# Down projection: 32 of its 44 K tiles as seven products over a sliding window of K pairs

## The chip, the cores and the metric

The kernel runs on one core of a Trainium2 chip. The metric is the device time of one execution in microseconds (us), from the first instruction to the last; the median of three runs is quoted. The five engines are named as in the profile: PE (matrix multiply, with its weight loads on a line of its own, PEld), DVE (vector), ACT (scalar), POOL (GpSimd) and SP, which issues most of the transfers.

## The reference, cut to what matters

One layer with two sub-layers is computed for 656 token columns (528 of one prompt stream with its meta tokens, 128 of eight sample streams), of which 640 reach the end. First come RMSNorm, an input projection, two mixers and an output projection; that part is not touched. Then comes the gated MLP:

```python
up = x @ w_up                       # 2048 -> 2 * 5632
g, v = up[..., :D_FF], up[..., D_FF:]
gc = conv_b
for k in range(FFN_CONV_W):         # depthwise causal conv, width 3
    gc = gc + gext[:, k:k + seqlen] * conv_w[k]
h = jax.nn.gelu(gc) * v
return h @ w_down                   # 5632 -> 2048
...
x = x + f                           # residual, then a final RMSNorm
```

In tiles of 128 the hidden width 5632 is 44 K tiles for `w_down`, and the output width 2048 is 16 row blocks n. Everything is float32; the products must be close to float32.

## The kernel before

**Products.** Each float32 operand is split into a rounded high part and a low rest (weights `wh` and `wl`, activations the same), and a product is three matmuls: wh with the high part, wh with the low part, wl with the high part. ACT writes the high part by a cast, DVE writes the low part by a subtraction. The 640 columns go as two halves of 320, so a weight tile costs six matmuls of 320 columns.

**The up projection** (`pu`, the stage ahead of the change) runs by Strassen's and Winograd's scheme: for each of 44 hidden tiles f, seven products (`CHAINS`: A11, P1, A22, P3, P2, A12, P4) over 8 pairs of K tiles replace eight. The activations stand ready in seven combinations (`B11, T1, B21, B22, T2, T3, T4`) in the tile `XT` for pairs 0 to 5 and in seven tiles `XH`, tags `xh0` to `xh6`, for pairs 6 and 7. A unit is half a chain: four weight tiles, 12 matmuls. Of the weights, A11, A21, A22 and A12 are loaded (`Up.load`), and DVE forms the sums P1, P3, P2, P4 (`Up.add`); the halves `wraw` and `wr` hold them. Cast and subtraction (`Up.split`) run three units ahead. Products are evicted by `evict_up`, then `gate` forms h of tile f on DVE and ACT, and POOL stores it to DRAM (`h_d`).

**The down projection** (`md` and `me`, the two names of its PSUM tiles) takes K tiles 0 to 39 in four chunks (`DCH`) of 11, 10, 10 and 9. For each chunk and n, six matmuls per K tile gather in PSUM, and `evict_down` adds the 640 columns into `acc`, which was loaded from `x3_d`, the residual rows in DRAM. `feed` reloads h tiles from `h_d` into a ring (`hida` in the seven `xh` tags, `hidb` in the space that `XT` had) and splits them.

**The tail** takes the last four K tiles (40 to 43) for column ranges of 384 and 256, adds, squares, normalises and stores. It stays as it is.

**Order.** Every engine runs its instructions in the order in which they were written out. The writing-out keeps a clock of its own (`E.now`, advanced by each matmul), and background generators (`E.spawn`, `E.tick`) place evictions, loads and splits where that clock says that their inputs are due. On the chip an engine, or a queue, that waits holds back all that stands behind it.

Of the kernel before, what the change touches and what calls it, by code (L numbers as in the profile page):

```python
# [16 lines left out]
DCH = [list(range(0, 11)), list(range(11, 21)), list(range(21, 31)), list(range(31, 40))]  # L17
# [26 lines left out]
def weight_order():  # L44
    o = []
    for k in range(KD):
        for n in range(4):
            o.append(("in", k, n))
    for n in range(4, 8):
        for k in range(KD):  # L50
            o.append(("in", k, n))
    for g in (3, 2, 1, 0):
        for n in (8 + 2 * g, 9 + 2 * g):
            for k in range(KD):
                o.append(("in", k, n))
# [32 lines left out]
    for k in DCH[0]:  # L88
        for n in range(4):
            o.append(("down", k, n))  # L90
    for c, ks in enumerate(DCH):
        for n in range(0 if c else 4, 16):
            for k in ks:
                o.append(("down", k, n))
# [9 lines left out]
B11, T1, B21, B22, T2, T3, T4 = range(7)  # L104
# [57 lines left out]
class Emit:  # L162
    def __init__(self, tc, A):
# [10 lines left out]
        self.limit = self.order.index(("down", 0, 0)) // CH  # L174
# [103 lines left out]
def body(tc, A):  # L278
# [40 lines left out]
    with tc.manual_schedule():  # L319
# [970 lines left out]
        UN = [(f, c, h) for f in range(NFF) for c in range(len(CHAINS)) for h in range(2)]  # L1290
# [3 lines left out]
        class Up:  # L1294
# [24 lines left out]

            def add(self, u):  # L1320
                if u >= len(UN):
                    return
# [3 lines left out]
                if p == "P1":  # L1326
                    if f:
                        self.put(f, "P1", h, "wraw")
                    else:
                        R[f, "P1", h] = r("A21")  # L1330
                    TT(r("P1"), r("A21"), r("A22"), ADD)
# [12 lines left out]
                if f == NFF - 1 and p == "P2" and h:  # L1344
                    E.limit = E.nchunk
                    for _ in range(4):
                        E.load_raw()

            def free(self, f, name, h):
                if f + 1 < NFF:  # L1350
# [5 lines left out]
            def hi(self, u):  # L1356
                if u < len(UN):
# [4 lines left out]
            def lo(self, u):  # L1362
                if u < len(UN):
# [16 lines left out]
        up.pool, up.later = None, []  # L1380
        pss = [mm4() for _ in range(2)]
# [60 lines left out]
        def f26():  # L1442
            return fpool[0].tile([128, 2 * XW], F32, tag="f26", name="f26", bufs=fpool[1])

        fpool = [None, 8]
# [6 lines left out]
        def gate(f, g, v, bufs=1):  # L1452
# [8 lines left out]
            gc, sq = f26(), f26()  # L1461
# [20 lines left out]
        def early(f, g, v):  # L1482
            while gating[0] < f:
                yield
            yield from gate(f, g, v)
            nc.gpsimd.dma_start(out=h_d[f], in_=v[:, 0:640])
            gating[0] += 1

# [4 lines left out]
        def evict_up(f, c):  # L1493
            a, d, e, cc, b = (PB.get((f, i)) for i in range(5))
            if c == 0:
                T_["m1"] = f7.tile([128, XW], F32, tag="m1", name="m1", bufs=1)
                S.copy(out=T_["m1"], in_=a[:, 0:XW])
            elif c == 4:
# [4 lines left out]
                v = T_["v"] = f26()  # L1503
# [3 lines left out]
                T_["done"] = f  # L1507
            elif c == 5:
                g = T_["g"] = f26().rearrange("p (a c) -> p a c", a=2)
                G.memset(g[:, 1, 320:322], 0.0)  # L1510
                TT(g[:, 0], b[:, 0:XW], T_["m1"], ADD)
            elif c == 6:
                g = T_["g"]
                TT(g[:, 1, 0:320], e[:, 0:320], T_["u2"], ADD)
                E.spawn(early(f, g, T_["v"]))
# [16 lines left out]
        def load_h(f):  # L1532
            hraw[f] = hidtile()
# [13 lines left out]

        mm = T.matmul
        for u, (f, c, h) in enumerate(UN):
            _, ty, bk, acc_ = CHAINS[c]  # L1550
            n = XW if ty in (B11, B21) else 320
# [25 lines left out]
            if u == len(UN) - 1:  # L1577
# [5 lines left out]
            for i in range(4):  # L1583
                k = 4 * h + i
                xh, xl = xkind(k, 0, ty)[:, 0:n], xkind(k, 1, ty)[:, 0:n]
                mm(out=p, lhsT=wh[:, i, :], rhs=xh, start=not acc_ and k == 0, stop=False, **more)
                mm(out=p, lhsT=wh[:, i, :], rhs=xl, start=False, stop=False, **more)
                mm(out=p, lhsT=wl[:, i, :], rhs=xh, start=False, stop=k == KP - 1, **more)
                E.tick()
            if h and u > 1:  # L1590
                E.spawn(evict_up(f, c), 0, True)
            if f == NFF - 1 and h and c < 6:
                load_h(c)
                E.spawn(first_h(c, E.now + 6))


        while (NFF - 1, 6) not in evicted:
# [10 lines left out]
        passed = [-1]  # L1608
        D = {}

        def feed():
            while gating[0] < NFF:
# [5 lines left out]
            fpool[1] = 8  # L1618
            D.update(cms=(cm_l1, cm_f8), acc=lps[0].tile([128, 16, 640], F32, name="acc"),
                     ssq=fpool[0].tile([128, 640], F32, name="ssq3"))  # L1620
            due = {}

            def load(f):
                if f < NFF:
                    while f - RING > passed[0]:
                        yield
                    load_h(f)
                    due[f] = E.now + 7

            for f in range(6, 9):  # L1630
                yield from load(f)
# [4 lines left out]
            for f in range(6, NFF):  # L1636
                yield from load(f + 3)
                yield from E.until(due[f])
# [22 lines left out]
        def down(c, ns):  # L1661
            ks = DCH[c]
            pss = {n: mm4() for n in ns}
            for k in ks:
                while k not in hid:
                    E.tick(True)
                for n in ns:
                    E.wtile(("down", k, n), pss[n][0], hid[k][:, 0], hid[k][:, 1], HP, k == ks[0], k == ks[-1])
            for n in ns:
                evict_down(n, pss[n][1])  # L1670

        for c, ks in enumerate(DCH):
            if c == 0:
                down(0, range(4))
            for n in range(0 if c else 4, 16):
                if c == len(DCH) - 1 and n == 12:
                    while NFF - 1 not in hid:
                        E.tick(True)
                down(c, [n])
            for k in ks:  # L1680
                hid.pop(k)
            passed[0] = ks[-1]
# [105 lines left out]
def _lay_out(x_prompt, x_sample, state_ssm_re, state_ssm_im, state_pool, state_ffn_conv,  # L1788
# [13 lines left out]
    for i, o in enumerate(order):  # L1802
        if o[0] == "pool":
            wts[i // CH, :, i % CH] = wp[o[1], o[2], :, o[3]]
        else:
# [4 lines left out]
                           for f in range(NFF) for k, n in ((0, 0), (0, NFF), (1, NFF), (1, 0))]).reshape(-1, 128, 4, 128)  # L1810
    xp = np.concatenate([meta_tokens, x_prompt[0]], axis=0)
# [52 lines left out]
```

## Time and profile before

| | us |
|---|---|
| median of three runs (2378.72 to 2382.51) | 2381.11 |
| the profiled execution | 2380.44 |
| its span on the core | 2378.7 |
| PE busy | 2335.2 |
| DVE busy | 1657.4 |
| ACT busy | 944.0 |
| POOL busy | 353.4 |

The span is what the profile sees of the profiled execution; 1.7 us of its time lie around it. The kernel has a first part of some 640 us with short waits, the up projection from 645.6 to 1739.9 us, the down projection from there to 2303.4 us, and a tail. Busy time of PE is a share of the span and says nothing of how fast single matmuls follow each other; that is read from how many start in a stretch.

### The profile page before, as it was taken

The page shows a single profiled execution, that of the slowest core. Times are in us where ns is not written, and L with a number is a line of the kernel's source. Part 1 is how long each engine was busy: PE and PEld are TensorE (multiplying, and loading weights), DVE is VectorE, ACT ScalarE, POOL GpSimd, SP SyncE. Part 2 cuts the span into 40 slices and gives each one's busy share as a digit, 9 for nine tenths or more (in the row PEclk, how much of TensorE's full clock was granted, in tenths as well). Part 3 has the DMA queues.
Part 4 walks back from the last instruction along what each step waited for, and adds up shares of the span by engine and source line. Part 5 has one row for each costly group of instructions (what it writes and reads, how often), then busy time and mean ns, then how long its engine had stood idle before and what let it go on. Part 6 is the DMA issues. An engine that isn't in the chain of part 4 may idle for free.

```text
span 2378.7 us, 41101 instructions
## 1 busy us (share of the span) xinstructions
PE 2335.2 (98%) x15824; PEld 2325.1 (98%) x15824; DVE 1657.4 (70%) x2709; ACT 944.0 (40%) x1644; POOL 353.4 (15%) x544
## 2 busy tenths in 40 slices
PE   9998989999999999999999999999999999999997
PEld 9998989989999999999999999999999999999997
DVE  7589888646788888888888888888872232422236
ACT  6233443334554444444444444444441221311125
POOL 4755534100000000000000000000000000000003
PEclk9999999999999999999999999999999999999999
DMA  6422345445433332333333333333364332422223
GB/s 189 121 80 81 106 139 163 142 126 163 155 105 106 95 108 89 100 107 94 108 90 100 107 93 109 90 100 107 93 225 148 96 116 72 131 76 76 76 80 111
DMA packets 151125, 265.93 MB, mean 112 GB/s; under 512 B 21008, under 2 KB 41616, under 8 KB 150928
## 3 DMA queue, kind: packets, MB, share of 16 engines
q1 hardware_dynamic: 144448, 248.10, 34.3%
q0 software_dynamic: 6336, 15.19, 2.3%
q8 instruction: 124, 2.03, 0.3%
q14 instruction: 73, 0.60, 0.1%
q10 hardware_dynamic: 144, 0.01, 0.0%
HBM read 225.10 MB, written 38.12 MB: 111 GB/s over the span
## 4 chain that ended last, share of the span: by engine, by line
PE 82%; DVE 2%; ACT 1%; issue 1%; POOL 0%; DMA 0%; SPq 0%; DVEq 0%; POOLq 0%; ACTq 0%
PE pu L159 45%; PE me L159 12%; PE md L159 12%; PE mm L159 9%; PE mf L159 2%; PE yps L159 1%; DVE f L132 1%; POOL ssq L132 0%; DVE wl L132 0%; DVE acc L132 0%; PE vps L159 0%; ACT f L132 0%; PE kp L159 0%; ACT wh L132 0%; DMA wr<-wup 0%
## 5 line engine op out<-in xcount | busy, mean ns | idle before, releaser
L159 PE MATMUL pu<-XT,wh 128*128 128x320 f32 (+1 forms) x3696 | 823.7, 310 | 0.5 <-DVE f L132 0.5
L159 PEld LDWEIGHTS pu<-XT,wh 128*128 128x128 f32 x3696 | 620.5, 189 | 0.9 <-issue 0.7
L132 ACT CAST wh<-wraw 128x512 fp32r<-128x512 f32 (+1 forms) x487 | 299.9, 617 | 728.4 <-PE md L159 220.2
L159 PE MATMUL pu<-XT,wl 128*128 128x320 f32 (+1 forms) x1848 | 572.5, 310 | 0.7 <-DVE wl L132 0.7
L132 DVE TENSOR_TENSOR wl<-wraw,wh 128x512 fp32r<-128x512 f32 (+1 forms) x487 | 339.3, 710 | 137.6 <-ACT wh L132 134.1
L132 ACT CAST wh<-wr 128x512 fp32r<-128x512 f32 x434 | 269.2, 621 | 406.5 <-PE pu L159 248.5
L159 PE MATMUL mm<-H,wh 128*128 128x320 f32 (+2 forms) x1920 | 374.6, 317 | 12.3 <-ACT H L132 8.4
L159 PEld LDWEIGHTS pu<-XT,wl 128*128 128x128 f32 x1848 | 349.4, 189 | 1.5 <-DVE wl L132 1.5
L132 DVE TENSOR_TENSOR wl<-wr,wh 128x512 fp32r<-128x512 f32 x434 | 298.2, 687 | 73.2 <-ACT wh L132 68.2
L159 PEld LDWEIGHTS mm<-H,wh 128*128 128x128 f32 x1920 | 306.1, 191 | 15.9 <-ACT H L132 8.6
L159 PE MATMUL pu<-XH,wh 128*128 128x320 f32 (+1 forms) x1232 | 277.2, 310 | 0.0
L159 PE MATMUL mm<-H,wl 128*128 128x320 f32 x960 | 223.5, 314 | 0.0
L159 PEld LDWEIGHTS pu<-XH,wh 128*128 128x128 f32 x1232 | 207.2, 189 | 0.0
L159 PE MATMUL pu<-XH,wl 128*128 128x320 f32 (+1 forms) x616 | 190.4, 309 | 0.0
L132 DVE TENSOR_TENSOR acc<-md,acc 128x640 f32<-128x640 f32 (+2 forms) x48 | 34.2, 712 | 193.5 <-PE md L159 193.5
L132 DVE TENSOR_TENSOR acc<-me,acc 128x640 f32<-128x640 f32 (+2 forms) x48 | 34.2, 712 | 192.1 <-PE me L159 192.1
L159 PEld LDWEIGHTS mm<-H,wl 128*128 128x128 f32 x960 | 164.5, 191 | 0.0
L159 PE MATMUL md<-hidb,wh 128*128 128x320 f32 x832 | 155.8, 309 | 0.0
L159 PE MATMUL me<-hidb,wh 128*128 128x320 f32 x832 | 155.8, 309 | 0.0
L159 PEld LDWEIGHTS me<-hidb,wh 128*128 128x128 f32 x832 | 130.8, 188 | 0.0
L159 PEld LDWEIGHTS md<-hidb,wh 128*128 128x128 f32 x832 | 130.8, 188 | 0.0
L132 DVE TENSOR_TENSOR wr<-wr 128x512 f32<-128x512 f32 x172 | 118.4, 689 | 2.8
(240 smaller groups left out, 3251.9 us busy)
## 6 DMA issues: line engine op xcount, KB each, us to landing
wraw<-wts SPq DMA_DIRECT2D x323, 256.0 KB, 2.7
wr<-wup SPq DMA_DIRECT2D x260, 256.0 KB, 3.0
wraw<-wup SPq DMA_DIRECT2D x90, 256.0 KB, 2.7
h_d<-f POOLq DMA_DIRECT2D x44, 320.0 KB, 2.5
hidb<-h_d SPq DMA_DIRECT2D x30, 320.0 KB, 4.7
w<-yg_d SPq DMA_DIRECT2D x16, 328.0 KB, 3.2
w<-xr SPq DMA_DIRECT2D x16, 322.0 KB, 3.7
x_d<-w SPq DMA_DIRECT2D x16, 322.0 KB, 3.9
```

The costliest lines, as they stand in the source:

```text
L132: return f(*a, **k)
L159: return self.eng.matmul(out=out, lhsT=lhsT, rhs=rhs, start=start, stop=stop, **more)
```

## The change

K tiles 0 to 31 of the down projection now run by the same scheme of seven products as the up projection. Four more (`HEAD`, 32 to 35) are multiplied in the old way right behind the up projection, and four (`REST`, 36 to 39) after the seven products. The tail keeps 40 to 43.

The 16 pairs of K tiles and the 8 pairs of row blocks give 16 steps s (units with f = 44 + s). Step s takes row blocks 2(s mod 8) and 2(s mod 8)+1 and the eight K pairs s to s+7 (mod 16), so each row pair is done in two steps, and from one step to the next one K pair leaves and one enters. The entering pair is built in the place of the leaving one in `XT` and `XH`: `load_pair` reads its two h tiles from `h_d`, `pair` forms the sums and splits all seven kinds. Pairs 0 to 5 are built while the last up tile and `HEAD` run, pairs 6 and 7 at the end of `HEAD` and in step 0 (`later_pairs`), whose units are reordered: five half chains over pairs 0 to 3 come first.

The sums go to DRAM instead of `acc`: `send` adds a row block of 640 columns to `x3_d[n]` by an accumulating DMA on POOL's queue, 16 from `HEAD` (`evict_head`, by ACT copies into the freed `xh` tiles) and 32 from the steps. From step 1 on the weight sum P1 is also made by DMA (`Up.sum`): SP loads A21, POOL's queue adds A22 onto it. `acc` is loaded after the last step.

```diff
-DCH = [list(range(0, 11)), list(range(11, 21)), list(range(21, 31)), list(range(31, 40))]
+NV2 = 16
+NU = NFF + NV2
+HEAD = list(range(32, 36))
+REST = list(range(36, 40))
...
+            def sum(self, f, name, half, a, b):
+
+                self.put(f, name, half, "wraw")
+                src = lambda n: A["wup"][(f * 4 + UP_LOADS.index(n)) * 2 + half]
+                SP.dma_start(out=R[f, name, half], in_=src(a))
+                nc.gpsimd.dma_start(out=R[f, name, half], in_=src(b), accum_op=ADD)
...
                 elif p == "P2":
                     TT(r("A11"), r("P1"), r("A11"), ADD)
                     R[f, "P2", h] = r("A11")
+                    if NFF <= f < NU - 1:
+                        self.sum(f + 1, "P1", h, "A21", "A22")
...
+        def send(n, t, hold):
+
+            yield from V.done()
+            nc.gpsimd.dma_start(out=x3_d[n], in_=half2(t[:, 0:640]), accum_op=ADD)
+            let(hold)
+            rows[0] += 1
...
+        def pair(p):
+            s, t = (p - KP, 0) if p >= KP else (-1, p)
+            x, y, hold, due = xy[p]
+            yield from past(s, 1, t)
+            yield from E.until(due)
+            e = G if p < KP + 2 else V
+            TT(x[:, 1], x[:, 0], x[:, 1], SUB, e)
+            yield from e.done()
+            yield from some(p, B11, x)
+            yield from past(s, 4, t)
+            if p != KP:
+                yield from V.idle()
+            STT(x[:, 1], x[:, 1], -1.0, y[:, 1], MUL, SUB)
+            TT(x[:, 0], x[:, 1], x[:, 0], ADD)
+            yield from V.done()
+            yield from some(p, T3, x)
+            TT(x[:, 1], x[:, 1], y[:, 0], ADD)
+            yield from V.done()
+            yield from some(p, T4, x[:, 1:2])
+            yield from past(s, 6, t)
+            yield from V.idle()
+            yield from some(p, B21, y, e)
+            let(hold)
+            built[0] += 1
...
+            for n in range(16):
+                while copied[0] < n - 2:
+                    E.tick(True)
+                ps = [bank1(), bank1()]
...
+                for i, k in enumerate(HEAD):
+                    while k not in hid:
+                        E.tick(True)
+                    E.wtile(("down", k, n), ps, hid[k][:, 0], hid[k][:, 1], HP, i == 0, i == len(HEAD) - 1)
...
+                E.spawn(evict_head(n, ps), 0, True)
...
+                j = (s + k) % KP if s >= 0 else k
+                while s >= 0 and have.get((j, ty)) != s + k:
+                    E.tick(True)
+                xh, xl = xkind(j, 0, ty)[:, 0:n], xkind(j, 1, ty)[:, 0:n]
...
         def feed():
-            while gating[0] < NFF:
+            while gating[0] < NFF or rows[0] < 16 + 2 * NV2:
                 yield
...
-                yield from E.until(t + 10 + 6 * (g - 4))
+                yield from E.until(t + 3 + 3 * (g - 4))
                 load_acc(g)
```

Counted over the whole program, PE has 15528 matmul instructions before and 15144 now.

**DVE, where the stage begins.** Before, behind the last eviction of the up projection, DVE runs the last gate (`gx`, `f`) and splits h tiles (`hida`) and weights for the first chunk:

```order
L132 TENSOR_TENSOR f_19645<-pu,u_19610 128x320
L132 TENSOR_TENSOR hida<-hida 128x640
L132 TENSOR_TENSOR gx<-f_19645,rstd 128x640
L132 TENSOR_TENSOR gx<-f_19645,rstd 128x2
L132 TENSOR_TENSOR wl<-wraw,wh 128x512
L132 TENSOR_TENSOR f_19623<-f_19623,rstd 128x640
```

Now, from the sum P1 for unit 6 of step 0 on, `f_20297` and `f_20298` being the two h tiles of pair 6, `f_20321` and `f_20322` those of pair 7, and `XH0b`, `XH1b` the new tiles of the kinds B11 and T1:

```order
L137 TENSOR_TENSOR wraw<-wr,wraw 128x512
L137 TENSOR_TENSOR wl<-wr,wh 128x512
L137 TENSOR_TENSOR XH0b<-f_20297,XH0b 128x320
L137 TENSOR_TENSOR XH0b<-f_20321,XH0b 128x320
L137 TENSOR_TENSOR wl<-wraw,wh 128x512
L137 TENSOR_TENSOR XH1b<-f_20297,XH1b 128x320
L137 TENSOR_TENSOR XH1b<-f_20321,XH1b 128x320
L137 SCALAR_TENSOR_TENSOR f_20297<-f_20297,f_20298 128x320
L137 TENSOR_TENSOR gx<-f_20297,f_20298 128x320
L137 TENSOR_TENSOR f_20297<-f_20297 128x320
```

The sums and low parts of pairs 6 and 7, twenty instructions of 320 columns in all, stand among the weight splits and sums of step 0.

**SP, from step 0 into step 1.** Before, the last up tile's weights are followed by h tiles for the ring and the first weights of the down projection:

```order
L1301 DMA wraw<-wup 128x512 x2
L1301 DMA wr<-wup 128x512 x6
L1534 DMA hida<-h_d_142 128x640
L1534 DMA hida<-h_d_143 128x640
L200 DMA wraw<-wts 128x512 x4
```

Now, with L1310 the plain loads of step 1's weights, L1333 the first operands of the two halves of its P1, and `f_20593`, `f_20594` the h tiles of pair 8:

```order
L1310 DMA wraw<-wup 128x512
L1333 DMA wraw<-wup 128x512
L1310 DMA wr<-wup 128x512
L1333 DMA wraw<-wup 128x512
L1310 DMA wr<-wup 128x512
L1628 DMA f_20593<-h_d_158 128x640
L1629 DMA f_20594<-h_d_159 128x640
L1310 DMA wr<-wup 128x512 x3
```

The last three weight loads of step 1 stand behind the load of pair 8's second tile.

**POOL, in the steady part.** Before, per up tile, the conv history in and out and the store of h:

```order
L1456 DMA gx<-chist 128x2x8
L1464 DMA cvo<-gx 128x2x9
L1486 DMA h_d_182<-f_18757 128x640
L132 MEMSET f_19072 128x2
L1456 DMA gx<-chist 128x2x8
```

Now, per step, two row sums into `x3_d` (L1531) and the second operands of P1 (L1334):

```order
L1531 DMA x_d_131<-f_21231 128x640
L1531 DMA x_d_130<-f_21260 128x640
L1334 DMA wraw<-wup 128x512 x2
L1531 DMA x_d_133<-f_21518 128x640
L1531 DMA x_d_132<-f_21547 128x640
```

Of the steps only the accumulating transfers are left on POOL's queue, each pair of weight sums ahead of the row sums of the step in which it is issued.

## Rows read from the trace of the kernel before

**Rows 1.** Page: the span, and busy time of each engine (us, share, instructions).

```profile
span 2378.7 us, 41101 instructions
PE 2335.2 (98%) x15824; PEld 2325.1 (98%) x15824; DVE 1657.4 (70%) x2709; ACT 944.0 (40%) x1644; POOL 353.4 (15%) x544
```

**Rows 2.** Page: the chain that ended last, shares of the span.

```profile
PE 82%; DVE 2%; ACT 1%; issue 1%; POOL 0%; DMA 0%; SPq 0%; DVEq 0%; POOLq 0%; ACTq 0%
```

**Rows 3.** Windows, steady up projection and down projection; columns as in the second line.

```profile
core 0: us, PE busy (x) PEld busy (x) DVE busy (x) ACT busy (x) POOL busy (x), PEclk, DMA share, GB/s
719.71:1739.90 1020.19, 1020.19 (x6913) 1020.19 (x6914) 892.91 (x1442) 476.40 (x827) 85.48 (x165) 1.00 0.35 101
1739.90:2303.40 563.50, 563.50 (x3841) 563.50 (x3841) 184.29 (x272) 127.73 (x206) 1.29 (x2) 1.00 0.34 108
```

**Rows 4.** Waits of PE from 640 to 1800 us: total, times, longest.

```profile
PE pu L159 <- DVE wl L132: 0.7, 1, 0.7
PE pu L159 <- DVE f L132: 0.5, 1, 0.5
```

**Rows 5.** Timeline of DVE, 1201 to 1215 us: start, length, instruction.

```profile
1201.38 0.68 DVE L132 TENSOR_TENSOR wr<-wr 128x512 f32<-128x512 f32 x1
1201.98 0.68 DVE L132 TENSOR_TENSOR wl<-wr,wh 128x512 fp32r<-128x512 f32 x1
...
1203.78 0.82 DVE L132 SCALAR_TENSOR_TENSOR f<-f,f 128x640 f32<-128x640 f32 x1
1204.52 0.68 DVE L132 TENSOR_TENSOR wr<-wraw,wr 128x512 f32<-128x512 f32 x1
...
1214.04 0.49 DVE L132 TENSOR_TENSOR f<-u,pu 128x320 f32<-128x320 f32 x1
1214.45 0.48 DVE L132 TENSOR_TENSOR f<-pu,u 128x320 f32<-128x320 f32 x1
```

**Rows 6.** Groups on ACT, 700 to 1700 us: busy, mean ns, idle before.

```profile
L132 ACT CAST wh<-wr 128x512 fp32r<-128x512 f32 x403 | 250.2, 621 | 384.2 <-PE pu L159 239.8 <-DVE wr L132 117.6 <-ACT f L132 13.0
L132 ACT COPY u<-pu 128x320 f32<-128x320 f32 x40 | 16.8, 421 | 0.0
```

**Rows 7.** DMA issues, 700 to 1700 us: count, size, median us to landing.

```profile
wr<-wup SPq DMA_DIRECT2D x242, 256.0 KB, 3.0
wraw<-wup SPq DMA_DIRECT2D x82, 256.0 KB, 2.7
h_d<-f POOLq DMA_DIRECT2D x40, 320.0 KB, 2.5
```

**Rows 8.** DMA from 1740 to 1800 us: total, the main queue, issues.

```profile
DMA packets 6566, 13.90 MB, mean 232 GB/s; under 512 B 752, under 2 KB 768, under 8 KB 6562
q1 hardware_dynamic: 6450, 13.51, 63.1%
...
hidb<-h_d SPq DMA_DIRECT2D x16, 320.0 KB, 5.6
wraw<-wts SPq DMA_DIRECT2D x18, 256.0 KB, 3.6
acc<-x_d SPq DMA_DIRECT2D x10, 320.0 KB, 5.0
```

**Rows 9.** Groups: POOL's arithmetic of nearby sizes, and its issue of a store.

```profile
L132 POOL TENSOR_TENSOR ct<-bc,npw 128x320 f32<-128x320 f32 x24 | 22.7, 961 | 0.6
L132 POOL TENSOR_TENSOR pa<-pz 128x630 f32<-128x630 f32 x6 | 11.2, 1868 | 24.2 <-ACT pz L132 24.1
L1486 POOL DMA_DIRECT2D h_d<-f x44 | 25.1, 571 | 473.1 <-DVE f L132 461.0 <-DVE wr L132 12.0
```

**Rows 10.** Windows, 0 to 300 us, all engines (columns as in rows 3).

```profile
0.00:300.00 300.00, 284.72 (x1930) 281.95 (x1931) 236.84 (x383) 121.59 (x221) 177.35 (x262) 0.98 0.39 115
```

**Rows 11.** Groups on DVE, the weight subtraction: 0 to 300 us, then 1740 to 2300.

```profile
L132 DVE TENSOR_TENSOR wl<-wraw,wh 128x512 fp32r<-128x512 f32 x67 | 56.5, 846 | 25.3 <-ACT wh L132 25.2
L132 DVE TENSOR_TENSOR wl<-wraw,wh 128x512 fp32r<-128x512 f32 x159 | 102.4, 684 | 1.2 <-ACT wh L132 1.2
```

More of the change, by code (lines that the diff above doesn't have):

```diff
@@ L87, in weight_order @@
             o.append(("out", k, n))
-    for k in DCH[0]:
+    for n in range(16):
+        for k in HEAD:
+            o.append(("down", k, n))
+    for k in REST:
         for n in range(4):
             o.append(("down", k, n))
[L91 to L94, printed above, removed]
+    for n in range(4, 16):
+        for k in REST:
+            o.append(("down", k, n))
     for ks, ns in tail_order(0):
@@ L99, in weight_order @@
     return o
-B11, T1, B21, B22, T2, T3, T4 = range(7)
+B11, T1, B21, B22, T3, T2, T4 = range(7)
 CHAINS = [("A11", B11, 0, False), ("P1", T1, 2, False), ("A22", T4, 1, False), ("P3", T3, 3, False),
@@ L1546, in first_h, with upos, past, load_pair @@
             yield from split_h(f)
+        have = {}
+        at = [-1000]
+        xy = {}
+        def upos(s, c, t):
+            return (s * len(CHAINS) + c) * KP + t
+        def past(s, c, t):
+            while at[0] <= upos(s, c, t):
+                yield
+        def load_pair(p):
+            hold = []
+            yield from room(2, True)
+            x, y = f26(hold), f26(hold)
+            SP.dma_start(out=x[:, 0:640], in_=h_d[2 * (p % NV2)])
+            SP.dma_start(out=y[:, 0:640], in_=h_d[2 * (p % NV2) + 1])
+            xy[p] = half2(x[:, 0:640]), half2(y[:, 0:640]), hold, E.now + 6
@@ new lines, in evict_head @@
+        def evict_head(n, ps):
+            hold = []
+            if n < 12:
+                while rows[0] < n - 5:
+                    yield
+                if n % 2 == 0:
+                    rowt[0] = xhp.tile([128, 2, 2 * XW], F32, tag=f"xh{(0, 5, 6)[n // 2 % 3]}", name="rowt", bufs=1)
+                t = rowt[0][:, n % 2]
+            else:
+                yield from room()
+                t = f26(hold)
+            for (o, w), p in zip(HP, ps):
+                S.copy(out=t[:, o:o + w], in_=p[:, 0:w])
+            copied[0] += 1
+            yield from S.done()
+            yield from send(n, t, hold)
@@ L1548, in body @@
         mm = T.matmul
         for u, (f, c, h) in enumerate(UN):
+            if u == U0:
+                up.end = len(UN)
+                head()
             _, ty, bk, acc_ = CHAINS[c]
-            n = XW if ty in (B11, B21) else 320
+            n = XW if ty in (B11, B21) and f < NFF else 320
+            s = f - NFF
+            if h == 0 and f == NFF:
+                while copied[0] < (14 if c == 0 else 16):
+                    E.tick(True)
             if h == 0 and not acc_ and (f, bk) not in PB:
@@ L1591, in body @@
                 E.spawn(evict_up(f, c), 0, True)
[L1592 to L1597, printed above, removed]
+            if f == NFF - 1 and h and 1 <= c <= 4:
+                load_h(HEAD[c - 1], xhp.tile([128, 2, 2 * XW], F32R, tag=f"xh{c}", name="hida", bufs=1))
+                E.spawn(first_h(HEAD[c - 1], E.now + 5.5))
+                if c == 1:
+                    for i in range(2):
+                        E.spawn(some_pairs([i, i + 2, i + 4]))
+                    E.spawn(later_pairs())
+            if f == NU - 1 and h and c < 6:
+                load_h(REST[0] + c)
+                E.spawn(first_h(REST[0] + c, E.now + 6))
+        while (NU - 1, 6) not in evicted:
             E.tick(True)
@@ L1618, in feed @@
             fpool[1] = 8
+            fl[0] = 0
+            live.clear()
             D.update(cms=(cm_l1, cm_f8), acc=lps[0].tile([128, 16, 640], F32, name="acc"),
                      ssq=fpool[0].tile([128, 640], F32, name="ssq3"))
[L1621 to L1631, printed above, removed]
             for g in range(4):
@@ L1635, in feed @@
             E.spawn(rest_acc())
-            for f in range(6, NFF):
-                yield from load(f + 3)
-                yield from E.until(due[f])
+            last = range(REST[0] + 6, NFF)
+            for f in last:
+                load_h(f)
+            yield from E.until(E.now + 7)
+            for f in last:
                 yield from split_h(f)
@@ L1667, in down @@
                 for n in ns:
-                    E.wtile(("down", k, n), pss[n][0], hid[k][:, 0], hid[k][:, 1], HP, k == ks[0], k == ks[-1])
+                    E.wtile(("down", k, n), pss[n][0], hid[k][:, 0], hid[k][:, 1], HP, k == REST[0], k == REST[-1])
             for n in ns:
                 evict_down(n, pss[n][1])
[L1672 to L1682, printed above, removed]
+        for k in REST:
+            hid.pop(k)
         acc, ssq = D["acc"], D["ssq"]
```

192 lines of the change are left out of this document (159 added, 33 removed).

## The prediction

> **What bounds the kernel now.** I read the page first: of 2378.7 us PE is busy 98%, the next engine, DVE, 70% [rows 1], and the chain that ended last is PE for 82% of the span [rows 2]. Busy shares of PE prove little, so next come the windows by stage. In the steady up projection 6913 matmuls start in 1020.19 us, 147.6 ns each; in the down projection 3841 in 563.50 us, 146.7 ns each; PE is busy in all of both, at a granted clock of 1.00, its upper level of 2.4 GHz [rows 3]. The waits of PE from 640 to 1800 us add up to 1.2 us [rows 4], and none is listed in the down projection. So in the stage that changes, time is the number of matmuls times their spacing, and everything else is hidden as long as it stays early. DVE shows how much room there is: 892.91 of 1020.19 us in the up projection (87.5%), 184.29 of 563.50 (33%) in the down projection [rows 3]. The change moves the second stage towards the first one's load.
>
> **What is removed.** Before, tiles 0 to 39 cost 40 x 16 x 6 = 3840 matmuls, 563.4 us at 146.7 ns. Now HEAD and REST cost 8 x 16 x 6 = 768, 112.7 us at the same spacing. The 16 steps cost 7 chains x 8 pairs x 3 = 168 matmuls each, 2688 in all. They are written like the up projection (`pu`, three matmuls for a weight tile), so I take 147.6 ns: 24.8 us a step, 396.7 us. The sum is 509.4 us, 54.0 less. The bound on the other side is 146.7 ns for the steps too: 56.3 less (384 matmuls fewer, as the order counts). The up projection mixes 322 and 320 columns, the steps have 320 throughout, so the truth should lie between.
>
> **The work of a step, and its cover.** Per step DVE has 14 weight subtractions and 6 weight sums of 512 columns, 3 splits of 640 (kinds B11/T1, T3/T2, B21/B22), and 10 instructions of 320: four sums, the split of T4, five for the evictions. Back to back DVE starts such instructions 0.60, 0.74 and 0.41 us apart [rows 5]: 12.0 + 2.2 + 4.1 = 18.3 us of 24.8, 74%. The up projection ran at 87.5% without PE waiting, since the gate, now gone, is dearer than the new splits. ACT has 14 casts of 0.62, two copies of 0.42 [rows 6] and casts of 2240 columns for the pair, some 3 us: 12.5 of 24.8. Both are free of charge as long as their inputs are early. A unit's split runs three units ahead of its use, 3 x 12 x 0.1476 = 5.3 us, and the entering pair is started in the chain behind the leaving one, with about five chains (18 us) until its first use. If this cover went, PE would wait in every step, and each microsecond would cost 16.
>
> **Transfers.** A step moves 12 pieces of 256 KB (8 loads, 2 x 2 for P1) and 4 of 320 KB (two h tiles in, two row sums), 4.46 MB, and reads 1.2 MB again to accumulate: 180 to 227 GB/s instead of 101 [rows 3]. The nearest row is the stretch from 1740 to 1800 us, 232 GB/s with the main queue at 63%: weights land there in 3.6 us [rows 8] instead of 3.0 [rows 7], and PE waits for nothing. The tightest weight load of a step, the next A11, is issued at the sum for P4, four units ahead of unit 12, and its cast follows unit 10, some 5 us later: 3.6 still fits, and the three units of lead stand behind that. Cost 0.
>
> **The accumulating transfer** is in no row. From below it costs what a store of 320 KB does, 2.5 us to landing [rows 7]; from above three such moves one behind the other (read, read, write), 7.5. I take 5, the time that `acc` loads of that size took in the busy stretch [rows 8]. POOL spends 0.57 us on issuing one [rows 9]. Where it is waited for: P1 of the next step is asked for when DVE has made P2, about nine units (15.9 us) before its cast. Take off 1 us of DVE lag, 0.3 of issue, 3.6 for the first load, 0.6 for the second issue: an accumulate may take 10.4 us. HEAD sends a row every 24 matmuls, 3.5 us, and has buffers for ten rows. So at 5 us nothing waits.
>
> **Where it is tight: step 0.** Call the end of HEAD zero. By the subtraction for step 1's first unit, due before 14 units x 1.77 = 24.8 us, DVE has 23 instructions of 512 and 20 of 320 columns, 22.0 us, and it can start on them only about 1 us before zero, while each of the seven kinds of pairs 6 and 7 also waits for two casts on ACT behind others. At unit 8 I count 13.3 us of DVE work against a need at 14.5. Then SP: the second tile of pair 8 can be loaded only when pair 6's second tile is split, at about 19 us, and A12 and the second half of A11 of step 1 are queued behind it; they land near 24 and are cast for a unit that starts at 26.6. I take 2 us of waiting, 0 to 8. POOL makes three differences of 320 columns there, 0.96 us each [rows 9]. What POOL does to DVE is shown by the first 300 us: with POOL busy 59% of the time [rows 10] the weight subtraction takes 846 ns, against 684 where POOL is idle [rows 11], 24% more. Over 3 us of POOL that is 0.7 us of DVE, inside the 2 us. The Trainium skill, page "SBUF — State Buffer", section "Who interferes with whom", is harsher: a VectorE instruction with two SBUF inputs contends with a GpSimd instruction that reads SBUF. If that meant waiting out each of the three, the total would come to about 2331 instead of 2329.
>
> **HEAD and REST.** While HEAD runs, DVE has some 54 instructions, about 30 of 56 us; POOL's ten in that time (1.87 us at 640 columns, 0.96 at 320 [rows 9]) stretch them by a few. The HEAD h tiles are loaded as chains 1 to 4 of the last up tile free their places; the last is issued one chain and a half before HEAD. I take 1 us, 0 to 4. After the last step `acc` waits for the last row sum: eviction 0.5, issue 0.6, accumulate 5, load 5.0 [rows 8], 11 us; the first four row blocks need it at about 13, when PE wants their banks for the fifth (96 matmuls, 14.1 us). Cost 0, up to 3 at 7.5 us an accumulate.
>
> **The sum.** Against the profiled execution, 2380.44: -54.0 + 2 + 1 = 2329.4 us, say 2329. The median of the runs is 2381.11, 0.7 higher, so the gain would be 2.2%.
>
> **Rivals.**
> - *The steps wait.* P1's sum lands late. Beyond 10.4 us each microsecond costs 15 (steps 1 to 15): at 12 us 15 x 1.6 = 24, total 2353. The same size comes from 1.5 us of any wait in each step, such as an h tile blocking ACT's queue. For it: SP and POOL must now go in turn, and POOL, waiting for SP's load, holds the row sums behind it. Against it: the margin is over twice the row that I lean on, and the row sums have a step to go. The Trainium skill, page "DMA: Bandwidth & Descriptors", section "Rules for kernel authors", wants just this order (an accumulating transfer must wait for the semaphore of the transfer that wrote its bytes); no run so far shows one.
> - *Accumulating is slow, and the kernel is slower than before.* If accumulates are served one after another at a us for 320 KB, a step needs 3.6a against 24.8, and the rows of HEAD must be out before their `xh` places are needed again, 12a + 7 against 78 us. At 7.5 that is 15 x 2.2 + 19 = 52 us, and the gain is gone; at 8 us, 15 x 4 + 25 = 85, total 2414. For it: nothing here has accumulated. Against it: 7.5 is three times the store [rows 7], with no overlap at all.
> - *The start is worse than I count*: step 0 and REST at their upper bounds, 8 + 4 + 3: 2341.
> - *The change does nothing for PE*: if matmuls of the steps were spaced wider, 20 ns more would eat the gain (2688 x 20 = 54 us). 41 tiles of the up projection in the same form say otherwise [rows 3].
>
> **How the numbers follow.** The forecast with its own bounds (2322 to 2335) 0.62; the start worse (2335 to 2343) 0.14; the steps wait (2343 to 2376) 0.15; accumulating slow, near or over the old time, 0.07; below 2322, by something that I don't see, 0.02. The range 2322 to 2352 takes in the first two cases and about half of the third, some 8 in 10. A measurement of this kernel tells about 0.2%, 4.8 us, from no change: faster (below 2376) 0.92, the same 0.03, slower 0.05.
>
> **What would show it.** Right: PE without gaps in the steps, one step every 24.6 to 24.8 us; DVE near 74% there; 384 matmuls fewer; waits of PE only within some 30 us of HEAD's end. Wrong: PE waiting for `wl` of P1 in each step with the cast waiting for the accumulate; accumulates landing in more than 10 us; SP held by h tiles in the steps; a gap of more than 8 us where HEAD ends; `acc` landing later than 14 us into REST.

## The result, and the profile after

The changed kernel takes 2354.55 us, median of four runs (2353.64 to 2358.56), beside 2380.91 for the kernel before on the same chip: a ratio of 0.9893 [0.9876, 0.991]. It is faster by 26 us. The forecast was 2329, the range 2322 to 2352: half of the expected gain is missing.

The profiled execution took 2358.56 us, the longest of the four. On the page (busy time by engine, and the chain that ended last) PE does less and DVE more than in [rows 1, 2], and a new name stands in the chain, DVE with 4%:

```profile
PE 2293.6 (97%) x15440; PEld 2276.6 (97%) x15440; DVE 1869.7 (79%) x3084; ACT 1060.2 (45%) x1879; POOL 442.9 (19%) x640
...
PE 78%; DVE 4%; issue 2%; ACT 1%; DMA 1%; POOL 0%; SPq 0%; DVEq 0%; POOLq 0%; ACTq 0%
```

Next the windows, as in [rows 3]: HEAD, step 0, steps 1 to 15 and REST, and then four stretches of 5 us. The columns are busy time of PE, PEld, DVE, ACT and POOL, granted clock, transfer share and rate.

```profile
1743.10:1809.00 65.90, 60.28 (x386) 59.29 (x385) 44.00 (x59) 34.75 (x73) 27.37 (x28) 0.95 0.76 186
1809.00:1845.00 36.00, 28.20 (x170) 26.20 (x169) 27.93 (x50) 16.41 (x35) 7.81 (x9) 0.91 0.66 161
1845.00:2225.20 380.20, 374.52 (x2522) 371.04 (x2521) 295.11 (x502) 179.47 (x312) 53.39 (x60) 1.00 0.72 173
2225.20:2281.80 56.60, 56.60 (x387) 56.60 (x386) 25.48 (x36) 12.98 (x21) 0.86 (x1) 1.00 0.61 190
...
1795.00:1800.00 5.00, 3.84 (x14) 3.85 (x15) 3.11 (x5) 0.00 (x0) 0.54 (x1) 0.54 0.56 171
1800.00:1805.00 5.00, 5.00 (x28) 5.00 (x28) 0.00 (x0) 0.00 (x0) 0.00 (x0) 0.77 0.57 199
1835.00:1840.00 5.00, 0.05 (x1) 0.08 (x1) 1.78 (x4) 0.94 (x2) 0.99 (x1) 0.64 1.06 361
1840.00:1845.00 5.00, 5.00 (x24) 5.00 (x25) 2.39 (x5) 1.87 (x3) 1.74 (x2) 0.68 0.74 169
```

HEAD should take 56.3 us and takes 65.9; step 0 should take 24.8 and takes 36.0; the 15 other steps should take 372.0 and take 380.2; REST takes what it should. So the loss is 9.6 + 11.2 + 8.2 = 29 us in this execution, against 3 in the forecast. The stage takes 538.7 instead of 563.5 us, and HEAD begins at 1743.1 instead of 1739.9: 2380.44 - 24.8 + 3.2 gives 2358.8, 0.3 from the measured time. Of the 3.2 us some 2 lie in the untouched first part, whose end differs by up to 5 us from run to run of all kernels here (the last store of `x` is issued between 647.3 and 652.2 us); no conclusion below hangs on them.

PE's timeline has the four gaps that are longest up to step 1 (start, length, instruction, and in brackets the idle time before it with what ended it):

```profile
1739.49 0.54 PE L164 MATMUL pu<-XT,wh 128*128 128x320 f32 x2 [1.75 <-DVE f L137]
...
1796.16 0.90 PE L164 MATMUL pu<-hida,wl 128*128 128x320 f32 x2 [4.76 <-DVE wl L137]
1810.80 0.41 PE L164 MATMUL pu<-XT,wl 128*128 128x320 f32 x1 [1.35 <-DVE wl L137]
...
1839.95 0.87 PE L164 MATMUL pu<-XT,wh 128*128 128x320 f32 x2 [5.93 <-DVE f L137]
```

Two of them cost twice. Behind the gaps of 4.76 and 5.93 us the granted clock is at its lower level, 1.2 GHz, for some microseconds (the mean of a 5 us window falls to 0.54 and 0.64). From 1796.2 to 1805 us PE starts 42 matmuls where 60 would fit at 147 ns, and from 1840 to 1845 us 24 where 34 would: 2.6 and 1.5 us more.

What stood in front of the gap at 1796 us is on DVE and POOL. First DVE's timeline:

```profile
1789.24 1.62 DVE L137 TENSOR_TENSOR f<-f,f 128x320 f32<-128x320 f32 x1
1790.79 5.31 DVE L137 TENSOR_TENSOR wl<-wraw,wh 128x512 fp32r<-128x512 f32 x1
1796.02 0.48 DVE L137 TENSOR_TENSOR XT<-f,XT 128x320 fp32r<-128x320 f32 x1
```

Then POOL's:

```profile
1775.84 2.55 POOL L137 TENSOR_TENSOR f<-f 128x320 f32<-128x320 f32 x3 [7.96 <-DMA f<-h_d]
...
1788.64 1.87 POOL L137 TENSOR_TENSOR XT<-f,XT 128x640 fp32r<-128x640 f32 x1 [2.54 <-ACT XT L137]
1790.47 0.86 POOL L1531 DMA_DIRECT2D x_d<-rowt  x1
1791.07 4.47 POOL L137 TENSOR_TENSOR XT<-f,XT 128x640 fp32r<-128x640 f32 x3
```

A weight subtraction of 0.69 us lasts 5.31: it ends at 1796.10, about its own length behind the end of POOL's run of three B21 splits (1791.07 + 4.47 = 1795.54). POOL is late with its work, since it had waited 7.96 us for an h tile before. On ACT two orders stand out:

```profile
1805.58 2.07 ACT L137 COPY f<-pu 128x320 f32<-128x320 f32 x6 [11.93 <-PE pu L164]
1807.48 0.68 ACT L137 CAST wh<-wr 128x512 fp32r<-128x512 f32 x1
...
1837.54 0.62 ACT L137 CAST wh<-wr 128x512 fp32r<-128x512 f32 x1 [3.30 <-DMA wr<-wup]
1838.06 0.42 ACT L137 COPY u<-pu 128x320 f32<-128x320 f32 x1
```

The first copies of HEAD's rows 12 to 14 stand in the order 14, 13, 12: ACT idles 11.9 us for row 14, with step 0's casts behind. At 1837.5 a cast for step 1 waits for its weights with the copy that empties a PSUM bank behind it; the bank comes free two DVE instructions later, and that is PE's gap of 5.93 us.

### The profile page after: what moved, and what is told of

It is laid out like the page before. It is cut to its first block, busy times and chain, and to the rows that moved or that the text cites. A ratio compares the mean times of both kernels' runs of the same rounds, so it can differ in the third digit from the quotient of the medians.

```text
span 2356.8 us, 41521 instructions
## 1 busy us (share of the span) xinstructions
PE 2293.6 (97%) x15440; PEld 2276.6 (97%) x15440; DVE 1869.7 (79%) x3084; ACT 1060.2 (45%) x1879; POOL 442.9 (19%) x640
## 4 chain that ended last, share of the span: by engine, by line
PE 78%; DVE 4%; issue 2%; ACT 1%; DMA 1%; POOL 0%; SPq 0%; DVEq 0%; POOLq 0%; ACTq 0%
PE pu L164 62%; PE mm L164 9%; PE mf L164 2%; PE me L164 2%; PE md L164 2%; DVE wl L137 1%; DVE f L137 1%; PE yps L164 1%; ACT wh L137 0%; POOL ssq L137 0%; ACT f L137 0%; DMA wr<-wup 0%; DVE acc L137 0%; PE vps L164 0%; DVE XT L137 0%
## 5 line engine op out<-in xcount | busy, mean ns | idle before, releaser
L164 PE MATMUL pu<-XT,wh 128*128 128x320 f32 (+1 forms) x5040 | 1125.1, 310 | 11.5 <-DVE f L137 8.2
L164 PEld LDWEIGHTS pu<-XT,wh 128*128 128x128 f32 x5040 | 847.4, 189 | 15.7 <-issue 10.2
L164 PE MATMUL pu<-XT,wl 128*128 128x320 f32 (+1 forms) x2520 | 781.9, 310 | 2.5 <-DVE wl L137 2.4
L137 ACT CAST wh<-wr 128x512 fp32r<-128x512 f32 x594 | 368.8, 621 | 543.6 <-PE pu L164 331.3
L137 DVE TENSOR_TENSOR wl<-wr,wh 128x512 fp32r<-128x512 f32 x594 | 411.8, 693 | 141.2 <-ACT wh L137 135.1
L164 PEld LDWEIGHTS pu<-XT,wl 128*128 128x128 f32 x2520 | 476.1, 189 | 4.4 <-DVE wl L137 4.4
L137 DVE SCALAR_TENSOR_TENSOR f<-f,f 128x640 f32<-128x640 f32 (+2 forms) x161 | 123.3, 766 | 2.6 <-ACT f L137 0.8
L164 PEld LDWEIGHTS pu<-XH,wl 128*128 128x128 f32 x616 | 116.4, 189 | 0.0
L137 DVE TENSOR_TENSOR wr<-wraw,wr 128x512 f32<-128x512 f32 x120 | 82.1, 684 | 0.1
L137 DVE SCALAR_TENSOR_TENSOR f<-gx,vec,f 128x640 f32<-128x640 f32 x88 | 78.8, 895 | 1.4
```

The source lines that it names most:

```text
L137: return f(*a, **k)
L164: return self.eng.matmul(out=out, lhsT=lhsT, rhs=rhs, start=start, stop=stop, **more)
```

## Theories

**A**: POOL's arithmetic stops DVE for its whole length, where the prediction took 24% of it. **B**: the h tiles of HEAD's pairs land late (a crowd of transfers), and their work bunches at HEAD's end, whoever does it. **C**: the reversed copies delay step 0. **D**: casts that wait for a transfer stand ahead of evictions on ACT. The rival to all of them is that DVE simply has too much work in HEAD and step 0, so that a wait removed comes back one place on.

| run | median us | ratio to before | HEAD us | steps us |
|---|---|---|---|---|
| changed kernel | 2354.55 | 0.9893 [0.9876, 0.991] | 66.0 | 416.1 |
| e1_dve | 2348.87 | 0.9866 [0.9849, 0.9882] | 59.2 | 413.5 |
| e2_inorder | 2351.34 | 0.988 [0.9865, 0.9895] | 64.5 | 412.4 |
| e3_dve_inorder | 2347.4 | 0.9862 [0.9848, 0.9877] | 60.3 | 412.5 |
| e4_poolall | 2357.08 | 0.9902 [0.9887, 0.9916] | 66.4 | 416.1 |
| e5_noacc | 2348.26 | 0.9865 [0.9851, 0.988] | 57.9 | 412.3 |
| e6_evictfirst | 2345.78 | 0.9853 [0.9836, 0.9869] | 64.7 | 406.0 |
| e7_three | 2340.51 | 0.9833 [0.9819, 0.9848] | 60.8 | 402.2 |
| e7b_uptoo | 2337.65 | 0.982 [0.9805, 0.9834] | 62.3 | 402.2 |
| e8_due | 2335.03 | 0.9807 [0.9792, 0.9821] | 56.7 | 402.5 |
| e9_due_noacc | 2335.72 | 0.9807 [0.9792, 0.9821] | 56.7 | 400.9 |
| e10_headplain | 2347.41 | 0.9856 [0.9839, 0.9872] | 57.9 | 415.4 |

The last two columns are from the profiled execution of each: from HEAD's first matmul to its last, and from there to REST's first. Four runs each; an interval is about 0.15% to either side, 3.5 us.

## The experiments

### POOL's arithmetic: e1_dve and e4_poolall

```diff
-            e = G if p < KP + 2 else V
+            e = V
...
-                TT(x[:, 1], x[:, 0], x[:, 1], SUB, G)
+                TT(x[:, 1], x[:, 0], x[:, 1], SUB)
```

> Every subtraction that the change gives to POOL (B11's difference and B21's low half of the entering pairs 0 to 5, 8 and 9, and B11's difference of pairs 6 and 7) goes to DVE; POOL keeps only DMA issues there. Theory A (a DVE instruction with two SBUF inputs stands until POOL's arithmetic ends): DVE instructions of 1.3 to 5.3 us between 1750 and 1812 us fall back to 0.5 to 0.8; the PE wait of 4.8 us near 1796 us and its time at the lower clock (about 4 us) go, the wait at 1811 shrinks: 8 to 12 us less than after, 2343 to 2347 by the median. Rival B (the h tiles of pairs 2 to 5 come late, and too much work stands at the end of the HEAD tiles, whoever does it): DVE gets about 20 more instructions, 11 us, in that stretch, the wait at its end stays or grows: 2353 to 2360.

The reverse dose, e4_poolall, has `e = G` for every pair.

> The reverse dose: POOL also makes the difference and the low half of B21 for pairs 10 to 22, one each in every step, 2.7 us of POOL a step. Theory A: DVE instructions beside them last until POOL is through, 0.5 to 2 us more each, twice a step: DVE's busy share in the steps rises from 74% to 78 to 84% although it has two instructions less; PE waits only where a weight subtraction is hit late: 0 to 1 us a step, 2354 to 2369. Rival, the mean of 24% on which the prediction leaned: DVE's share falls by some 3 points (1.3 us less work, 0.65 us lost of 24.8), and the time stays, 2353 to 2356.

e1_dve is 5.7 us faster by the median, less than A asked (7.5 at least). In the profiled execution HEAD is 6.8 us shorter and the steps 2.6, but HEAD begins 2.1 us later (1745.2): the gap ahead of it is 2.88 us instead of 1.75, and behind it the granted clock is at 0.50 to 0.54 up to 1744 us. PE's timeline shows what is left of the gap of 4.76 us:

```profile
1779.14 0.56 PE L164 MATMUL pu<-hida,wl 128*128 128x320 f32 x2 [1.44 <-DVE wl L137]
1783.53 0.56 PE L164 MATMUL pu<-hida,wl 128*128 128x320 f32 x2 [0.60 <-DVE wl L137]
```

In HEAD the subtractions `wl<-wraw` take 686 ns now, against 1052 in the changed kernel. The rest is B: DVE now waits for the h tiles as POOL did before, with a weight subtraction behind:

```profile
1777.19 1.30 DVE L137 TENSOR_TENSOR f<-f 128x320 f32<-128x320 f32 x3 [6.36 <-DMA f<-h_d]
1778.40 0.69 DVE L137 TENSOR_TENSOR wl<-wraw,wh 128x512 fp32r<-128x512 f32 x1
```

In e4_poolall the same 330 us of the steps read, in the windows view, as

```profile
1870.00:2200.00 330.00, 326.36 (x2198) 323.33 (x2197) 264.83 (x413) 154.79 (x270) 79.62 (x82) 1.00 0.74 175
```

beside this row of the changed kernel:

```profile
1870.00:2200.00 330.00, 326.49 (x2199) 323.47 (x2198) 256.25 (x440) 155.17 (x271) 46.91 (x54) 1.00 0.74 176
```

DVE has 27 instructions fewer (half of 320, half of 640 columns: by [rows 5] some 27 x 0.58 = 16 us) and is busy 8.6 us longer, while POOL works 32.7 us more. So POOL's 32.7 us cost DVE 16 + 8.6 = 24 us, three quarters; at 24% it would be 8. That decides for A, against the mean of 24%. PE does not notice: 2198 matmuls against 2199, and the medians differ by less than the intervals. So a stop of DVE costs time only where it hits a subtraction without lead, one that PE needs as soon as it is done.

### The order of the copies: e2_inorder and e3_dve_inorder

```diff
         def evict_head(n, ps):
             hold = []
+            while copied[0] < n:
+                yield
```

> The ACT copies of the HEAD rows 12 to 15 are made to go in order, so that no copy of row 14 stands on ACT ahead of row 12's and 13's. Theory C: the idle time of 11.9 us on ACT before 1805.6 us goes, step 0's first casts come earlier, and the PE wait of 1.35 us at 1811 goes; as the wait of 4.8 us before it and the one of 5.9 us at 1840 have other causes, 1 to 3 us less than after: 2352 to 2354. Rival: the start of step 0 is set by DVE anyway: no change, 2354 to 2355.

> Both edits at once. If A and C hold and add up: 9 to 14 us less than after, 2340 to 2346. If the wait at 1840 us (weights of step 1 in a crowd of transfers) also came from DVE being late in step 0, it goes too with its time at the lower clock: 16 to 20 us less, 2335 to 2339. If neither holds: 2353 to 2360.

ACT's timeline of e2_inorder has a cast between the copies, and PE has no gap where the changed kernel has the one at 1811 us:

```profile
1798.33 0.76 ACT L137 COPY f<-pu 128x320 f32<-128x320 f32 x2 [7.39 <-PE pu L164]
1798.97 0.63 ACT L137 CAST wh<-wr 128x512 fp32r<-128x512 f32 x1
1802.12 0.76 ACT L137 COPY f<-pu 128x320 f32<-128x320 f32 x2 [2.52 <-PE pu L164]
```

But e1_dve, whose copies are still reversed, has no such gap either (0.71 us at 1817 is the first in step 0). In the changed kernel the subtraction that PE waits for there lasts 2.56 us; DVE's line of it, then POOL's work beside it:

```profile
1808.19 2.56 DVE L137 TENSOR_TENSOR wl<-wr,wh 128x512 fp32r<-128x512 f32 x1 [10.08 <-ACT wh L137]
```

```profile
1808.51 2.94 POOL L137 TENSOR_TENSOR f<-f 128x320 f32<-128x320 f32 x2
```

So this wait needed both, the reversed copies and POOL's stop, and C alone is not shown as its cause. The time of e2_inorder, 3.2 us less, is no larger than the intervals, and e3_dve_inorder adds only 1.5 to e1_dve. Together they miss what was expected. The wait near 1840 us is 6.0 us in e2_inorder, 3.6 in e1_dve and 5.0 in e3_dve_inorder: its size changes, but it does not go with A or C.

### Evictions ahead of casts: e6_evictfirst

```diff
-            up.add(u + 4)
-            if u:
-                up.split(u + 3)
+            late = f >= NFF
+            if not late:
+                up.add(u + 4)
+                if u:
+                    up.split(u + 3)
...
                 E.tick()
+                if late and i == 2:
+                    up.add(u + 4)
+                    up.split(u + 3)
```

> Only the order in the steps changes: the next weights' sum, cast and subtraction are written behind the third weight tile of a unit instead of ahead of its first, so that a cast whose weights are still on their way no longer stands on ACT ahead of the copy that empties a PSUM bank. Theory D (the wait of 5.9 us at 1840 us is that cast, held by a transfer in the crowd of step 1's loads): the wait goes or falls below 3 us, with most of the stretch at the lower clock behind it: 4 to 9 us less than after, 2345 to 2350. Rival: the weights themselves are late, PE waits for them a unit later for as long: 2352 to 2357. A cast in steady steps has half a unit less lead; if that was needed, PE waits for wh or wl in every step and it is slower than after, over 2360.

This is the largest single gain, 8.8 us; the steps are 10 us shorter. ACT's timeline shows the copy ahead of the cast that waits:

```profile
1834.08 0.42 ACT L137 COPY u<-pu 128x320 f32<-128x320 f32 x1
1838.47 0.62 ACT L137 CAST wh<-wr 128x512 fp32r<-128x512 f32 x1 [3.98 <-DMA wr<-wup]
```

The weights are as late as before (3.98 us of waiting on ACT), PE waits 1.79 us instead of 5.93, and the clock stays at 1.00. So D made some 4 of the 5.9 us, and the lateness itself no more than the rest. The edit also gave something that no theory had named. A stretch of steps 8 to 13 of the changed kernel, in the windows view,

```profile
2035.00:2170.00 135.00, 134.52 (x909) 133.36 (x908) 104.34 (x177) 63.74 (x108) 19.14 (x22) 1.00 0.75 178
```

and of e6_evictfirst:

```profile
2035.00:2170.00 135.00, 135.00 (x919) 135.00 (x919) 104.38 (x181) 64.73 (x112) 19.17 (x22) 1.00 0.75 182
```

Ten matmuls more in the same time: the weight loads of the changed kernel pause 0.3 us once a step (5 times, 1.6 us in all, in this stretch), where on DVE the evictions of a unit stand behind a weight subtraction and two instructions of the entering pair. Over 16 steps (397 us) that is 397/135 x 10 x 0.147 = 4.3 us, about half of what this run gained.

### Together, and on to a faster version: e7_three, e7b_uptoo, e8_due

e7_three joins e1, e2 and e6. e7b_uptoo has `late = f >= NFF - 1` besides, and e8_due also

```diff
-            xy[p] = half2(x[:, 0:640]), half2(y[:, 0:640]), hold, E.now + 6
+            xy[p] = half2(x[:, 0:640]), half2(y[:, 0:640]), hold, E.now + (12 if p < KP - 2 else 6)
```

> The three edits together (POOL's arithmetic on DVE, copies in order, evictions ahead of the next casts in the steps). If A, C and D are separate causes that add up: 7 us less from the first two, 4 to 9 from the third: 2338 to 2344. If the wait at 1840 us only moves: 2346 to 2350.

> As the three together, with the order also changed in the last up tile, where PE waits 1.8 to 2.9 us near 1739 us for the same kind of copy behind a cast whose h tile is still on its way: 1 to 3 us less than the three together, 2336 to 2342; if the wait only moves, the same as the three.

> The four edits that e7b_uptoo had, and one number: work on the HEAD pairs' h tiles is written 12 us behind their loads instead of 6, so that a subtraction that waits for a late h tile (5.1 us on DVE near 1773 us in e7b_uptoo) no longer stands ahead of a weight subtraction. If that wait is the rest of what HEAD loses, the PE wait of 2.6 us and some 3 us at the lower clock go: 4 to 6 us less than e7b_uptoo, 2332 to 2334. Rival: the pairs' work only moves into step 0, which is full on DVE: 2336 to 2341.

e7_three is 14.0 us below the changed kernel, where 7.2 (e3) and 8.8 (e6) add up to 16: the causes are separate, and the rival of a wait that only moves is out. e7b_uptoo gains 2.9 us, within the intervals; its gap near 1737 us is 1.7 us instead of 2.8, but in e8_due, with the same order there, it is 3.3. So that part is not settled. e8_due is 2.6 us below e7b_uptoo, less than the 4 to 6 expected and within the intervals; its median lies between the two expectations. But HEAD is now without a gap, where e7b_uptoo had one of 2.58 us: the windows of HEAD, the steps and REST, and of 330 us in the steps.

```profile
1746.10:1802.80 56.70, 56.70 (x388) 56.70 (x387) 42.84 (x73) 35.32 (x74) 14.14 (x17) 1.00 0.90 217
1802.80:2205.30 402.50, 399.11 (x2690) 397.21 (x2689) 315.78 (x555) 194.17 (x346) 53.28 (x62) 1.00 0.73 178
2205.30:2262.00 56.70, 56.70 (x388) 56.70 (x387) 25.50 (x37) 13.01 (x21) 0.85 (x1) 1.00 0.60 189
...
1860.00:2190.00 330.00, 330.00 (x2244) 330.00 (x2243) 256.00 (x447) 157.44 (x276) 45.57 (x53) 1.00 0.73 178
```

HEAD takes 56.7 us (56.3 forecast), a steady step 168 x 330/2244 = 24.7 us (24.8 forecast). Left are PE gaps of 1.7 and 1.4 us around the start of step 1, the second with about 1.5 us lost at the lower clock behind it (17 matmuls from 1843 to 1847 us, where 27 would fit), and the one of 3.3 us ahead of HEAD. At 2335.03 us this version beats both kernels. Its stage sums up to 515.9 us against 512.4 in the forecast (509.4 + 2 + 1).

### What accumulating costs: e5_noacc, e10_headplain, e9_due_noacc

In e5_noacc both `accum_op=ADD` are gone, in e10_headplain that of HEAD's 16 rows alone; e9_due_noacc is e8_due without either.

> The transfers that accumulate become plain stores and loads (the row sums and the weight sum P1 lose their first term): what accumulating itself costs. Prediction's view: it is waited for nowhere, 0 to 2 us less than after (fewer bytes in the crowd near 1835 us), 2352 to 2355. Rival, accumulating on the path: a microsecond or more in each step, 2340 or less, with issue times on POOL of 0.57 instead of 0.87 us.

> The changed kernel with only the 16 rows of HEAD stored plainly (their residual term is lost); the steps' rows and P1 still accumulate. If the 6.3 us of e5_noacc lie in HEAD (accumulates there land in 7.1 us and hold the transfer engines, h tiles and weights land later), the same gain: 2347 to 2351, with the wait of 4.8 us near 1796 us gone or under 1. If they lie in the steps (P1), no gain: 2353 to 2355.

> e8_due with plain stores and loads in place of the accumulating ones (the row sums and P1 lose their first term): whether accumulating still costs anything once the three other causes are gone. If the 6.3 us of e5_noacc came only through the crowd that made h tiles and weights late at the two bunched places, 0 to 2 us less than e8_due; if accumulating costs time by itself, 5 us or more.

The first expectation was a miss: 6.3 us less, not 0 to 2. e10_headplain gains 7.1 us, and by its profile in HEAD (66.0 to 57.9 us; the steps stay at 415.4, the gap near 1840 us at 6.1). In e5_noacc HEAD is as short, but the steps are 3.8 us shorter too, with 3.4 us of gap near 1840 us: whether plain loads of P1 thin out that crowd is open, since the medians of the two runs differ by less than the intervals. The transfers from 1745 to 1800 us of the changed kernel (queues: packets, MB, share of 16 engines; then issues with their time to landing):

```profile
q0 software_dynamic: 1840, 4.27, 46.0%
q1 hardware_dynamic: 3303, 6.67, 36.5%
...
x_d<-rowt POOLq DMA_DIRECT2D x12, 320.0 KB, 7.1
f<-h_d SPq DMA_DIRECT2D x12, 320.0 KB, 7.0
wraw<-wts SPq DMA_DIRECT2D x11, 256.0 KB, 6.1
```

and the same stretch, counted from HEAD's start, of e10_headplain:

```profile
q0 software_dynamic: 1103, 4.43, 21.4%
...
x_d<-rowt POOLq DMA_DIRECT2D x12, 320.0 KB, 3.7
f<-h_d SPq DMA_DIRECT2D x12, 320.0 KB, 5.3
wraw<-wts SPq DMA_DIRECT2D x11, 256.0 KB, 3.4
```

Accumulating, POOL's queue holds the transfer engines more than twice as long for about the same bytes, and h tiles and weights land 1.7 to 2.7 us later. That is the crowd of B. POOL's heap of B21 splits stands in e10_headplain too and stretches a weight subtraction to 4.95 us, but a later one, and PE waits 0.52 us. So the gap at 1796 us needed both, the late tiles and POOL's stop, and taking away either takes most of it: 6.8 us of HEAD by the one, 8.1 by the other. In e9_due_noacc, where POOL's arithmetic and the heap are gone, plain transfers gain nothing (0.7 us more, within the intervals). So no cost of accumulating by itself shows, within the intervals of 3.5 us.

## Why the prediction was wrong

**Right: the bound and the main term.** 384 matmuls fewer at the old spacing are worth 54 us; a steady step without gaps takes 24.7 us, REST 56.6. DVE's share in the steps is 256.25 of 330 us, 78% against 74%, and covers them. An accumulate lands in 4.3 to 4.5 us by the page of the changed kernel (taken as 5), though in 7.1 in HEAD, where the waits list none for it either, and PE waits for P1 in no step: the rivals of a late P1 and of slow accumulates are out, and so is the rival of a wider spacing, but for 0.3 us a step.

**The failed step: HEAD and step 0, forecast at 1 us (0 to 4) and 2 us (0 to 8), measured 9.6 and 11.2.** Both lie beyond the bounds. The rival of a worse start is the case that came, but it had 12 us at most for the two, against 20.8. By the number alone, 2354.55 lies in the bracket of the rival that the steps wait (2343 to 2376); that is chance, since steps 1 to 15 lost 8.2 of the 29 us, and none of it at P1. What made the loss in HEAD and step 0:

- *POOL's stop.* The 24% was a mean over 300 us [rows 10, 11] of two kinds: in the trace of the kernel before 47 of the 67 subtractions last 0.63 to 0.77 us, and 20 last 0.80 to 2.09, all 20 beside POOL's arithmetic (lines below). Taken as a rate it made "a few" microseconds of ten long instructions; in truth one subtraction lost 4.6 us. In HEAD DVE's 59 instructions take 44.0 us, where the 69 in e1_dve take 40.6, 0.59 each: some 9 us of stretch, as an estimate from these two means. Of HEAD's excess e1_dve takes 6.8 us away. The Trainium skill, page "SBUF — State Buffer", section "Who interferes with whom", calls the shared port pair an exclusive lock, and says that a VectorE instruction with two SBUF inputs contends with a GpSimd instruction that reads SBUF. The prediction weighed it, for three instructions of step 0 alone, and gave it 2 us. The runs agree with the harsher reading (5.31 us beside 4.47 of POOL; three quarters in e4_poolall). By it the ten in HEAD had to be asked for the lead of the subtraction that each can hit, since a run of three is longer (4.47 us) than PE's 3.5 us with one chunk of weights (24 matmuls). The longest of the 20, in the kernel before, and POOL's instruction beside it:

```profile
155.34 2.09 DVE L132 TENSOR_TENSOR wl<-wraw,wh 128x512 fp32r<-128x512 f32 x1
```

```profile
154.94 1.94 POOL L132 TENSOR_TENSOR pa<-pz 128x630 f32<-128x630 f32 x1 [3.27 <-ACT pz L132]
```

- *Accumulates in HEAD.* The margin was worked out for who waits on an accumulate, and that held. The transfers beside it were left out: an accumulate takes engine time from the h tiles, which come late already, since SP stands 15.94 us on HEAD's weights ahead of them:

```profile
1743.08 15.94 SPq L206 DMA_DIRECT2D wraw<-wts  x6
1759.20 0.34 SPq L1628 DMA_DIRECT2D f<-h_d  x1
```

- *The wait at 1840 us.* Its place was named (pair 8's tiles ahead of step 1's weights), and the weights were late as feared: cast 28.5 and 31.1 us after step 0's start, not near 24. But the prediction asked only when the unit that needs them begins, and not what stands behind the waiting cast on ACT: an eviction, due a unit earlier. It named ACT's queue only in the rival that every step waits (blocked by an h tile), not at this place. e6_evictfirst shows that this order is worth 4 of the 5.9 us, with the clock behind it.
- *The clock.* No term had it. Each of the two long gaps has a stretch at 1.2 GHz behind it, 2.6 and 1.5 us.
- *The wait of 1.35 us at 1811 us*, unseen. It disappears with the copies in order (e2_inorder), and also without POOL's arithmetic (e1_dve), so it needed both.
- *DVE without slack in step 0*, what the 2 us were meant for, came to about 1.2 us: PE's weight loads pause four times between 1824 and 1829 us, by 0.23 to 0.43 us each, for a cast or a subtraction.

**Unnamed: 8.2 us in steps 1 to 15.** The 0.3 us a step is 4 of them, shown by e6_evictfirst; the listed waits of PE make up the rest, 1.4 us at 1857 and others of 0.7 to 1.0.

**Open.** The gap of 1.3 to 3.3 us at the end of the last up tile stands in every run. In the changed kernel a cast of `hida` waits 2.63 us for its h tile ahead of the copy of `u`, as in D. The order that cured the steps did not cure it, but it moves only the weights' casts: in e7b_uptoo the cast of `hida` still stands ahead of the copy, and waits longer. Moving that cast was not tried.

```profile
1733.04 0.73 ACT L137 CAST hida<-hida 128x640 fp32r<-128x640 f32 x1 [3.77 <-DMA hida<-h_d]
...
1734.19 0.42 ACT L137 COPY u<-pu 128x320 f32<-128x320 f32 x1
```

## What to carry to other kernels

Ask of each instruction that can wait for a transfer not only who needs its result, but what stands behind it in the order of its engine; an eviction behind a waiting cast cost PE some 4 of 5.9 us here. A mean over a long stretch is no price for an instruction that is hit or not: price the worst single one, against the lead of the work that it stops. Moving arithmetic from DVE to POOL freed nothing here, where both read SBUF beside each other: in e4_poolall three quarters of POOL's time came out of DVE's.

## What the runs showed of the hardware

- An accumulating transfer of 320 KB lands in 4.5 us (median of 36), one of 256 KB in 4.3 (of 30), and POOL is busy 0.87 us with its issue, against 2.5 us and 0.57 for the plain store of 320 KB. In HEAD it takes 7.1 us against 3.7, and the queue's share of the engines is 46.0% for 4.27 MB against 21.4% for 4.43 MB.
- A DVE subtraction of 512 columns, 0.69 us alone, lasted 5.31 us beside three POOL instructions in a row and ended 0.56 us behind the last: by these times DVE got no turn between them.
- Behind the gaps of 4.8 and 5.9 us PE ran at the lower clock. Behind short gaps it came out both ways, so the length of a gap alone does not tell: in e6_evictfirst the granted clock stayed at 1.00 behind 1.79 us (at 1836 us) and was 0.50 from 1740 to 1742 us, soon behind 1.80 us (at 1738.5 us); behind 1.44 us it stayed at 1.00 in the changed kernel (1857 us) and fell to a mean of 0.54 over 2 us in e8_due (1843 us).
